# Both token halves of the next slice's gate and up projections ahead of each down-projection group, equal groups in both layers, and silu as one activation

## The chip, the cores and the metric

The kernel runs on one core of one Trainium2 chip. The metric is the device time of one execution in microseconds (us): the median of a few runs. Besides, one execution was recorded by the hardware profiler, and every row below is from that one. The engines are named as the profile names them: PE is the matrix engine (TensorE) and PEld its weight loads, DVE is VectorE, ACT is ScalarE, POOL is GpSimd, SP is SyncE, which here does nothing but issue transfers.

## What is computed

Two layers of a diffusion trunk over 640 tokens (512 latent, 128 of context) of width 1024. In each layer a conditioning vector gives six rows of shifts, scales and gates (the modulation); three kinds of mixers follow, an output projection, and a feed-forward block:

```
m  = silu(c) @ w_mod + b_mod                       # 6 rows of 1024 per conditioning vector
x  = layernorm(ALPHA * x + gate1 * mixers(modulated x) @ w_out)
h2 = layernorm(x) * (1 + scale2) + shift2
y  = (silu(h2 @ w_gate) * (h2 @ w_up)) @ w_down     # inner width 2816
x  = layernorm(ALPHA * x + gate2 * y)
```

The modulation takes a row each for two conditioning vectors (latent and context tokens).

## The kernel before

**Tiling.** The inner width of the feed-forward block is cut into 22 slices of 128. A matrix product in fp32 is made of three PE instructions on high and low parts (`mm3`, lines 218 to 220). Weights come in by SP transfers of 512 KB into `wraw` (line 211); ACT makes the high part `whi` (line 205), DVE the low part `wlo` (line 206). There are eight slots for such weight pairs.

**One slice.** `gu_unit(f, h)` makes the gate and up projection of slice `f` for one half of the tokens: 256 tokens (h = 0) or 384 (h = 1), 48 matmuls into two PSUM banks `pg` and `pu`. Before, silu takes two steps: ACT writes sigmoid(pg) into `sg` (line 1184), DVE multiplies it by `pg` (line 1185). DVE then multiplies by `pu` (line 1186). Behind h = 1 ACT and DVE split the slice's `sg` (640 tokens) into `ah` and `al`, and the slice's down weights are fetched.

**One group.** The slices are worked in groups (`GROUPS`). Behind the gate and up projections of a group stand its down projections: `d_unit(gi, t, hs)` for token tiles t = 0 to 4, each of two column halves `dps` of 512 columns, 3 matmuls for each slice and half. A finished half is multiplied by a gate row (line 1086, `residual`) and added to the residual `xr` (line 1088 in the first group, 1090 in later ones). All matmul outputs rotate through eight PSUM banks, so a unit that wants a bank waits until what it held has been evicted.

**Gate rows.** The first down unit of a layer fetches them (`gates(1)`, line 1071) from `gd` in DRAM, which the modulation writes: `modulation` works through pieces of 128 x 512 of the modulation weights. For each piece SP fetches `wm` (line 282), DVE multiplies and sums it for one conditioning vector (line 308), POOL multiplies it for the other (line 312), and ACT sums that product (line 288). Behind the last piece of a part DVE forms `modV` (lines 318, 319) and POOL issues the write of `gd` (line 323). Part 5 is the gate of the feed-forward block.

**Order.** PE runs in the order in which the program lists the matmuls. Units are listed by hand; the modulation's pieces are woven in between by a planner (`Order`), which lets one pass per so many planned microseconds of PE work (the pace). The order on ACT, DVE, POOL and SP follows from that by a scheduler. Before, layer 0 works its own part 5 (16 pieces, pace 2.8) and then parts 0 to 4 of layer 1 (80 pieces, pace 3.4) during its feed-forward block; layer 1 works its own part 5 (16 pieces, pace 2.8) during its own.

Of the kernel before, what the change touches and what calls it, by code (L numbers as in the profile page):

```python
# [12 lines left out]
AF = mybir.ActivationFunctionType  # L13
ALU = mybir.AluOpType
# [3 lines left out]
T = 640  # L18
NK = 8
NFF = 22  # L20
GROUPS = (((0, 4), (4, 4), (8, 4), (12, 4), (16, 6)), ((0, 5), (5, 6), (11, 5), (16, 6)))
ALPHA = float((2 * L) ** 0.25)
EPS = 1e-5
P = dict(pf=(0,), hf=0, hf4=2, vr0=1.0, vr=3.0, ew=5, lm=(0, 0), beg=12.0, dve=7.9, pace0=2.8, pace1=2.8, pace2=(3.4, 2.8), r=6.5, b=6.5, lev=2.4, v=6.1, hn=2.9, mixm=6.0, co=3.5, rco=4.0, rcs=3.0, norm=3.0)
HALVES = ((0, 256), (256, 384))
HH = (slice(0, 512), slice(512, 1024))
SWAP16 = [i ^ 16 for i in range(32)]
# [7 lines left out]
class Slots:  # L35
# [46 lines left out]
    def again(self, t, name, shape, dt=F32):  # L82

        kind, i, _ = self.held.pop(id(t))
        return self.view(kind, i, name, shape, dt)
# [66 lines left out]
class Kernel:  # L152
# [114 lines left out]
    def modulation(self, l, which, pace, dve):  # L267

        nc = self.nc
        keep = self.tc.keep_in_program_order  # L270
        again = self.mem.again
        yield lambda: self.can(ax=5 if dve else 6)
        csb = [self.get("ax", "csb", (128, 512)) for _ in range(2)]
        wts = deque(self.get("ax", "wm", (128, 512)) for _ in range(3 if dve else 4))
        acc = self.const.tile([128, 6, 2, 2, NK], F32, name="acc", tag="acc", bufs=1)
        ahead, tails = deque(), deque()

        def load(h, n, k):
            wt = again(wts.popleft(), "wm", (128, 512))
            wts.append(wt)  # L280
            r0 = (which[n] * NK + k) * 128
            keep(nc.sync.dma_start(wt, self.a["w_modT"][l, r0:r0 + 128, h * 512:(h + 1) * 512]))
            ahead.append((h, n, k, wt))

        def finish_tails(left):
            while len(tails) > left:
                t, d = tails.popleft()
                keep(nc.scalar.activation(out=t, in_=t, func=AF.Copy, accum_out=d))  # L288

        for h in range(2):  # L290
            for s in range(2):
                csb[s] = again(csb[s], "csb", (128, 512))
                nc.sync.dma_start(csb[s], self.a["crow"][s, h * 512:(h + 1) * 512].unsqueeze(0).to_broadcast([128, 512]))
                j = again(wts.popleft(), "junk", (128, 512))
                wts.append(j)
                nc.scalar.activation(out=j, in_=csb[s], func=AF.Sigmoid)
                nc.vector.tensor_tensor(csb[s], csb[s], j, ALU.mult)
                yield -pace
            pieces = deque((h, n, k) for n in range(len(which)) for k in range(NK))
            for _ in range(len(wts) - 2):  # L300
                load(*pieces.popleft())
            while ahead:
                if pieces:
                    load(*pieces.popleft())
                yield -pace
                _, n, k, wt = ahead.popleft()
                d = [acc[:, n, h, s, k:k + 1] for s in range(2)]
                keep(nc.vector.scalar_tensor_tensor(self.jb, wt, 1.0, csb[0], ALU.mult, ALU.mult, accum_out=d[0]))  # L308
                if dve:
                    nc.vector.scalar_tensor_tensor(self.jb, wt, 1.0, csb[1], ALU.mult, ALU.mult, accum_out=d[1])  # L310
                else:
                    nc.gpsimd.tensor_tensor(wt, wt, csb[1], ALU.mult)  # L312
                    tails.append((wt, d[1]))
                    finish_tails(1)
            finish_tails(0)
        for n, w in enumerate(which):
            v = self.modV[:, l, w]
            nc.vector.tensor_tensor(v, acc[:, n, 0], acc[:, n, 1], ALU.add)
            nc.vector.tensor_tensor(v, v, self.bmf[:, l, w].unsqueeze(1).to_broadcast([128, 2, NK]), ALU.add)
            if w in (1, 4):  # L320
                nc.vector.tensor_scalar(v, v, 1.0, None, ALU.add)
            if w in (2, 5):
                nc.gpsimd.dma_start(self.gd[l, w // 3].rearrange("s (k f) -> f (s k)", f=128),
                                    v.rearrange("p s k -> p (s k)"))
        self.free(*csb, *wts)
        self.mark(("mod", l, which[-1]))
# [100 lines left out]
    def tm_out(self, l, g, t, ps, n):  # L427
        self.mark(("V", l, g, t), P["v"])
        for j in range(n):
# [29 lines left out]
    def mixers(self, l, hT, mp):  # L459
        nc, a, o = self.nc, self.a, self.o  # L460
# [31 lines left out]
        hn = [[("hT", l, 0), ("hT", l, 1)], [("hT", l, 2), ("hT", l, 3), ("hT", l, 4)]]  # L492
# [50 lines left out]
        def e_unit(i, h):  # L543
            ps = half(15 + i, h, "pgt", 0)
            c0, n = HALVES[h]
            if h == 0:
                self.sg[i] = self.m4("sg", (128, T))
            sg = self.sg[i]
            nc.scalar.activation(out=sg[:, c0:c0 + n], in_=ps[:, :n], func=AF.Sigmoid)
            nc.vector.tensor_tensor(sg[:, c0:c0 + n], sg[:, c0:c0 + n], ps[:, :n], ALU.mult)  # L550
            if h:
                nc.vector.tensor_tensor(sg, sg, self.raws[i], ALU.mult)
                self.free(self.raws[i])
                m = 5 + i if i < 3 else i - 1
                self.mix[m] = (self.ax("mh"), self.ax("ml"))
                self.split(sg, *self.mix[m])
                self.free(sg)
                self.mark(("mix", l, m), P["mixm"])
# [497 lines left out]
    def feed(self, l, fp):  # L1056
        nc, a, o = self.nc, self.a, self.o
# [104 lines left out]
        par1 = []  # L1162

        def later_modulation():
            yield lambda: ("gu", l, P["lm"][l]) in self.at
            if l == 0:
                yield from self.modulation(0, (5,), P["pace1"], False)
            yield from self.modulation(1, (5,) if l else range(5), P["pace2"][l], False)

        o.start(later_modulation())  # L1170
        hT = self.hts("hT") if l < L - 1 else None
        acts, wd, sgs, wgu = {}, {}, {}, {}
        hn = [[("h2", l, 0), ("h2", l, 1)], [("h2", l, 2), ("h2", l, 3), ("h2", l, 4)]]

        def gu_unit(f, h):
            if f not in wgu:
                wgu[f] = (self.loadw(a["w_gate"][l, f]), self.loadw(a["w_up"][l, f], eng=nc.gpsimd if f in P["pf"] else None))
                sgs[f] = fp.tile([128, T], F32, tag="sg", name="sg", bufs=1)
            c0, n = HALVES[h]
            pg = self.fm_half(wgu[f][0], h2, h, "pg")  # L1180
            pu = self.fm_half(wgu[f][1], h2, h, "pu")
            self.mark(("gu", l, f))
            sg = sgs[f][:, c0:c0 + n]
            nc.scalar.activation(out=sg, in_=pg[:, :n], func=AF.Sigmoid)
            nc.vector.tensor_tensor(sg, sg, pg[:, :n], ALU.mult)
            nc.vector.tensor_tensor(sg, sg, pu[:, :n], ALU.mult)
            if h:
                for w in wgu.pop(f):
                    self.free(*w)
                acts[f] = (self.ax("ah"), self.ax("al"))  # L1190
                self.split(sgs[f], *acts[f])
                wd[f] = self.loadw(a["w_down"][l, f * 128:(f + 1) * 128, :])

        def d_unit(gi, t, hs):
            f0, n = GROUPS[l][gi]
            if not g2:
# [9 lines left out]
            if t == 4 and 1 in hs:  # L1206
                for f in range(f0, f0 + n):
                    self.free(*wd.pop(f), *acts.pop(f))
            final = gi == len(GROUPS[l]) - 1
            with self.tc.high_priority(offset=2000 if final else 0):  # L1210
# [14 lines left out]
        def gu(f, h):  # L1225
            self.unit(lambda: gu_unit(f, h), hn[h] + ([("gu", l, f)] if h else []), 5.2 if h == 0 else 7.8,
                      {"W": 2} if h == 0 else {"ax": 2})

        for gi, (f0, n) in enumerate(GROUPS[l]):


            if gi == 0 or l:
                gu(f0, 0)
            gu(f0, 1)
            for f in range(f0 + 1, f0 + n):
                for h in range(2):
                    gu(f, h)
            if gi < len(GROUPS[l]) - 1:
                if l == 0:
                    gu(f0 + n, 0)  # L1240
                for t in range(5):
                    self.unit(lambda gi=gi, t=t: d_unit(gi, t, (0, 1)), [("mod", l, 5)], 0.0)
                self.run_units(ahead=4 if gi == 0 else 1)
        self.run_units(ahead=1)
        gi = len(GROUPS[l]) - 1
        if l < L - 1:
# [238 lines left out]
```

## Time and profile before

| | |
|---|---|
| median of three runs | 1785.79 us (1784.29 to 1786.83) |
| the profiled execution, whole | 1783.5 us |
| its span, first to last instruction | 1781.7 us |
| mean granted TensorE clock over the span | 0.983 of full speed |
| PE busy | 1690.5 us, 95% of the span |
| DVE, ACT, POOL busy | 64%, 38%, 25% |

The profiled execution lies 2.3 us under the median. Its first gate projection starts at 433.3 us in layer 0 and at 1297.3 us in layer 1. An engine's busy share over the whole span does not say what an edit is worth; what PE waits for in the stretch that the edit touches does.

### The profile page before, as it was taken

The numbers are of one execution on the slowest core, as the hardware profiler recorded it, in microseconds if no ns is written. First come the engines' busy times: TensorE is split into PE (matmuls) and PEld (weight loads), VectorE is DVE, ScalarE is ACT, GpSimd is POOL, SyncE is SP. The second block draws the span as 40 slices with busy tenths as digits, with TensorE's granted clock in tenths as the row PEclk, the third lists the DMA queues.
The fourth block names the chain that finished last, engine by engine and source line by source line (L and its number), as shares of the span: only waits on it lengthen the run. The fifth ranks groups of instructions, "written<-read, shape, count | busy, mean of one in ns | idle before, by whom it ended". The sixth has DMA issues, their size and how long they took to land.

```text
span 1781.7 us, 29207 instructions
## 1 busy us (share of the span) xinstructions
PE 1690.5 (95%) x11634; PEld 1548.7 (87%) x11634; DVE 1134.1 (64%) x1979; ACT 671.3 (38%) x1277; POOL 452.4 (25%) x461
## 2 busy tenths in 40 slices
PE   6989879999888999999999999999999899999998
PEld 4878778888878999989989998879798799898996
DVE  4497897658657775877394546675767533434427
ACT  4623332735433443434254434256354122221310
POOL 2223342103253443543042333220233100000001
PEclk9999989999999999999999999999999899999999
DMA  8444521243345453544223122113244332221311
GB/s 327 156 131 132 144 61 40 81 166 95 102 147 166 154 166 119 174 122 154 72 82 120 60 62 69 40 58 117 100 137 146 108 103 71 73 84 47 106 36 59
DMA packets 71497, 195.47 MB, mean 110 GB/s; under 512 B 11953, under 2 KB 12737, under 8 KB 71361
## 3 DMA queue, kind: packets, MB, share of 16 engines
q1 hardware_dynamic: 67392, 183.15, 32.3%
q0 software_dynamic: 3680, 10.35, 1.8%
q8 instruction: 91, 1.49, 0.3%
q14 instruction: 46, 0.37, 0.1%
q10 hardware_dynamic: 288, 0.11, 0.0%
HBM read 187.52 MB, written 6.06 MB: 109 GB/s over the span
## 4 chain that ended last, share of the span: by engine, by line
PE 56%; DVE 5%; issue 3%; ACT 2%; DMA 2%; POOL 1%; DVEq 0%; ACTq 0%; POOLq 0%
PE dps L220 5%; PE dps L219 5%; PE dps L218 5%; PE pg L220 4%; PE pg L219 4%; PE pg L218 4%; PE pu L218 4%; PE pu L220 4%; PE pu L219 4%; PE pl L819 1%; PE p L218 1%; PE p L220 1%; PE p L219 1%; DVE jb L308 1%; DVE wlo L206 1%
## 5 line engine op out<-in xcount | busy, mean ns | idle before, releaser
L206 DVE TENSOR_TENSOR wlo<-wraw,whi 128x1024 fp32r<-128x1024 f32 x204 | 262.0, 1287 | 228.0 <-ACT whi L205 226.9
L205 ACT CAST whi<-wraw 128x1024 fp32r<-128x1024 f32 x206 | 215.3, 1048 | 431.7 <-PE pg L219 110.0
L312 POOL TENSOR_TENSOR wm<-wm,csb 128x512 f32<-128x512 f32 x112 | 182.4, 1644 | 263.9 <-DVE jb L308 255.3
L220 PE MATMUL pg<-h2T,wlo 128*128 128x384 f32 (+1 forms) x704 | 218.4, 310 | 2.4 <-DVE wlo L206 2.4
L218 PE MATMUL pg<-h2T,whi 128*128 128x384 f32 (+1 forms) x704 | 218.7, 311 | 0.0
L219 PE MATMUL pg<-h2T,whi 128*128 128x384 f32 (+1 forms) x704 | 218.0, 310 | 0.0
L218 PE MATMUL pu<-h2T,whi 128*128 128x384 f32 (+1 forms) x704 | 217.6, 309 | 0.0
L220 PE MATMUL pu<-h2T,wlo 128*128 128x384 f32 (+1 forms) x704 | 217.6, 309 | 0.0
L219 PE MATMUL pu<-h2T,whi 128*128 128x384 f32 (+1 forms) x704 | 217.6, 309 | 0.0
L218 PE MATMUL dps<-whi,ah 128*128 128x512 f32 x440 | 175.3, 399 | 17.0 <-ACT ah L205 11.7
L220 PE MATMUL dps<-whi,al 128*128 128x512 f32 x440 | 174.7, 397 | 3.4 <-DVE al L206 3.4
L219 PE MATMUL dps<-wlo,ah 128*128 128x512 f32 x440 | 174.4, 396 | 0.0
L334 POOL TENSOR_SCALAR bnve<-bnag 128x1 f32<-128x1 f32 x40 | 14.7, 371 | 596.3 <-DVE bnag L332 521.8
L308 DVE SCALAR_TENSOR_TENSOR jb<-wm,csb 128x512 bf16<-128x512 f32 x160 | 154.1, 963 | 11.2 <-DMA wm<-in_w_modT 9.3
L288 ACT ACTIVATE wm<-wm 128x512 f32<-128x512 f32 x112 | 70.7, 631 | 189.8 <-POOL wm L312 189.7
L220 PEld LDWEIGHTS pg<-h2T,wlo 128*128 128x128 f32 x704 | 134.0, 190 | 3.0 <-DVE wlo L206 3.0
L218 PEld LDWEIGHTS pg<-h2T,whi 128*128 128x128 f32 x704 | 134.1, 191 | 0.3
L219 PEld LDWEIGHTS pg<-h2T,whi 128*128 128x128 f32 x704 | 134.1, 190 | 0.3
L218 PEld LDWEIGHTS pu<-h2T,whi 128*128 128x128 f32 x704 | 133.8, 190 | 0.0
L219 PEld LDWEIGHTS pu<-h2T,whi 128*128 128x128 f32 x704 | 133.8, 190 | 0.0
L220 PEld LDWEIGHTS pu<-h2T,wlo 128*128 128x128 f32 x704 | 133.8, 190 | 0.0
L1086 DVE TENSOR_TENSOR dps<-dps,gate 128x512 f32<-128x512 f32 x90 | 60.8, 695 | 101.1 <-PE dps L220 71.1
(270 smaller groups left out, 3854.2 us busy)
## 6 DMA issues: line engine op xcount, KB each, us to landing
wm<-in_w_modT SPq DMA_DIRECT2D x160, 256.0 KB, 2.9
wraw<-in_w_gate SPq DMA_DIRECT2D x44, 512.0 KB, 3.6
wraw<-in_w_up SPq DMA_DIRECT2D x44, 512.0 KB, 3.7
wraw<-in_w_down SPq DMA_DIRECT2D x44, 512.0 KB, 3.6
wraw<-in_w_fm SPq DMA_DIRECT2D x42, 512.0 KB, 3.6
wm<-in_w_mod SPq DMA_DIRECT2D x16, 512.0 KB, 10.2
wraw<-in_w_tm SPq DMA_DIRECT2D x16, 512.0 KB, 3.7
wraw<-in_w_out SPq DMA_DIRECT2D x16, 512.0 KB, 3.7
```

Source lines behind the costliest of these rows:

```text
L205: self.nc.scalar.copy(hi, raw)
L206: (eng or self.nc.vector).tensor_tensor(lo, raw, hi.bitcast(F32), ALU.subtract)
L218: mm(out, lh, rh, start=first, stop=False)
L219: mm(out, lh, rl, start=False, stop=False)
L220: mm(out, ll, rh, start=False, stop=last)
L288: keep(nc.scalar.activation(out=t, in_=t, func=AF.Copy, accum_out=d))
L308: keep(nc.vector.scalar_tensor_tensor(self.jb, wt, 1.0, csb[0], ALU.mult, ALU.mult, accum_out=d[0]))
L312: nc.gpsimd.tensor_tensor(wt, wt, csb[1], ALU.mult)
L334: nc.gpsimd.tensor_scalar(ve, ag[:, 1:2], EPS, None, ALU.add)
L819: nc.tensor.matmul(pl[hh][:, u * 128:(u + 1) * 128], C[p0:p0 + 64, u * 128:(u + 1) * 128], pick(Qf, p0, p0 + 64, u * 128, [[2 * s, 64 // s ...
L1086: nc.vector.tensor_tensor(ps, ps, gt[:, HH[h]], ALU.mult)
```

## The change

Three things are done at once.

1. **Order and groups.** In both layers both halves of the next group's first slice now stand ahead of a group's down projections; before, layer 0 had only h = 0 there, and layer 1 neither. Layer 1 takes layer 0's groups, 4, 4, 4, 4 and 6 slices in place of 5, 6, 5 and 6.
2. **Modulation.** Part 5 of layer 1 is worked in layer 0 as well. Layer 0 now weaves in 16 + 96 pieces, the last 96 at a pace of 3.0, and layer 1's feed-forward block none.
3. **Silu.** ACT makes silu in one activation, in place of sigmoid on ACT and a multiplication on DVE, at three places: the gate projection, the mixers' output gates (`e_unit`) and the conditioning vector in the modulation that is woven in.

```diff
-GROUPS = (((0, 4), (4, 4), (8, 4), (12, 4), (16, 6)), ((0, 5), (5, 6), (11, 5), (16, 6)))
+GROUPS = (((0, 4), (4, 4), (8, 4), (12, 4), (16, 6)), ((0, 4), (4, 4), (8, 4), (12, 4), (16, 6)))
...
-P = dict(pf=(0,), hf=0, hf4=2, vr0=1.0, vr=3.0, ew=5, lm=(0, 0), beg=12.0, dve=7.9, pace0=2.8, pace1=2.8, pace2=(3.4, 2.8), r=6.5, b=6.5, lev=2.4, v=6.1, hn=2.9, mixm=6.0, co=3.5, rco=4.0, rcs=3.0, norm=3.0)
+P = dict(pf=(0,), hf=0, hf4=2, vr0=1.0, vr=3.0, ew=5, lm=0, beg=12.0, dve=7.9, pace0=2.8, pace1=2.8, pace2=3.0, r=6.5, b=6.5, lev=2.4, v=6.1, hn=2.9, mixm=6.0, co=3.5, rco=4.0, rcs=3.0, norm=3.0)
...
-                j = again(wts.popleft(), "junk", (128, 512))
-                wts.append(j)
-                nc.scalar.activation(out=j, in_=csb[s], func=AF.Sigmoid)
-                nc.vector.tensor_tensor(csb[s], csb[s], j, ALU.mult)
+                if dve:
...
+                else:
+                    nc.scalar.activation(out=csb[s], in_=csb[s], func=AF.Silu)
...
-            nc.scalar.activation(out=sg[:, c0:c0 + n], in_=ps[:, :n], func=AF.Sigmoid)
-            nc.vector.tensor_tensor(sg[:, c0:c0 + n], sg[:, c0:c0 + n], ps[:, :n], ALU.mult)
+            nc.scalar.activation(out=sg[:, c0:c0 + n], in_=ps[:, :n], func=AF.Silu)
...
-            yield lambda: ("gu", l, P["lm"][l]) in self.at
+            yield lambda: ("gu", l, P["lm"]) in self.at
             if l == 0:
                 yield from self.modulation(0, (5,), P["pace1"], False)
-            yield from self.modulation(1, (5,) if l else range(5), P["pace2"][l], False)
-
-        o.start(later_modulation())
+                yield from self.modulation(1, range(6), P["pace2"], False)
+
+        if l == 0:
+            o.start(later_modulation())
...
-            nc.scalar.activation(out=sg, in_=pg[:, :n], func=AF.Sigmoid)
-            nc.vector.tensor_tensor(sg, sg, pg[:, :n], ALU.mult)
+            nc.scalar.activation(out=sg, in_=pg[:, :n], func=AF.Silu)
             nc.vector.tensor_tensor(sg, sg, pu[:, :n], ALU.mult)
...
-            if gi == 0 or l:
-                gu(f0, 0)
-            gu(f0, 1)
-            for f in range(f0 + 1, f0 + n):
+            ending = gi == len(GROUPS[l]) - 1
+            for f in range(f0 + (gi > 0), f0 + n + (not ending)):
                 for h in range(2):
                     gu(f, h)
-            if gi < len(GROUPS[l]) - 1:
-                if l == 0:
-                    gu(f0 + n, 0)
+            if not ending:
                 for t in range(5):
```

**PE, layer 0, in front of the first down projection.** Each row is one instruction with its line, its output, its inputs and the output's shape. Before, the last matmuls ahead of it are those of slice 4's first half (256 columns):

```order
L218 MATMUL pu<-h2T_4040,whi 128x256
L219 MATMUL pu<-h2T_4041,whi 128x256
L220 MATMUL pu<-h2T_4040,wlo 128x256
L218 MATMUL dps<-whi,ah 128x512
L219 MATMUL dps<-wlo,ah 128x512
L220 MATMUL dps<-whi,al 128x512
```

Of the change, at the same place:

```order
L218 MATMUL pu<-h2T_4028,whi 128x384
L219 MATMUL pu<-h2T_4029,whi 128x384
L220 MATMUL pu<-h2T_4028,wlo 128x384
L218 MATMUL dps<-whi,ah 128x512
L219 MATMUL dps<-wlo,ah 128x512
L220 MATMUL dps<-whi,al 128x512
```

The 48 matmuls of slice 4's second half moved from behind the group's down projections to ahead of them; the number of matmuls in the program is the same.

**DVE, layer 0, in front of the first eviction of a down projection** (`dps<-dps,gate`). Before:

```order
L206 TENSOR_TENSOR wlo<-wraw,whi 128x1024
L206 TENSOR_TENSOR al<-sg,ah 128x640
L1185 TENSOR_TENSOR sg<-sg,pg 128x256
L1186 TENSOR_TENSOR sg<-sg,pu 128x256
L308 SCALAR_TENSOR_TENSOR jb,acc<-wm,csb 128x512 x3
L297 TENSOR_TENSOR csb<-csb,junk 128x512
L318 TENSOR_TENSOR modV<-acc 128x16
L319 TENSOR_TENSOR modV<-modV,bmf 128x16
L297 TENSOR_TENSOR csb<-csb,junk 128x512
L1086 TENSOR_TENSOR dps<-dps,gate 128x512 x2
L1088 SCALAR_TENSOR_TENSOR xr<-xr,dps 128x512 x2
```

Of the change (its line numbers are 2 or 3 higher there):

```order
L206 TENSOR_TENSOR wlo<-wraw,whi 128x1024
L206 TENSOR_TENSOR al<-sg,ah 128x640
L1188 TENSOR_TENSOR sg<-sg,pu 128x256
L311 SCALAR_TENSOR_TENSOR jb,acc<-wm,csb 128x512 x3
L321 TENSOR_TENSOR modV<-acc 128x16
L322 TENSOR_TENSOR modV<-modV,bmf 128x16
L206 TENSOR_TENSOR wlo<-wraw,whi 128x1024
L1188 TENSOR_TENSOR sg<-sg,pu 128x384
L206 TENSOR_TENSOR wlo<-wraw,whi 128x1024
L206 TENSOR_TENSOR al<-sg,ah 128x640
L1088 TENSOR_TENSOR dps<-dps,gate 128x512 x2
L1090 SCALAR_TENSOR_TENSOR xr<-xr,dps 128x512 x2
```

The same three pieces still stand behind slice 4's first half and ahead of `modV`; the multiplications by `pg` and by `junk` are gone, and slice 4's second half, its split and two weight splits stand between `modV` and the first eviction.

**SP, layer 1, ahead of the gate rows.** Before:

```order
L211 DMA wraw<-in_w_gate 128x1024
L282 DMA wm<-in_w_modT 128x512 x3
L211 DMA wraw<-in_w_up 128x1024
L211 DMA wraw<-in_w_down 128x1024
L293 DMA csb<-in_crow 128x512 x2
L282 DMA wm<-in_w_modT 128x512 x8
L211 DMA wraw<-in_w_gate 128x1024
L211 DMA wraw<-in_w_up 128x1024
L1071 DMA gate<-gd 128x1024 x2
```

Of the change:

```order
L211 DMA wraw<-in_w_down 128x1024 x4
L211 DMA wraw<-in_w_gate 128x1024
L211 DMA wraw<-in_w_up 128x1024
L211 DMA wraw<-in_w_down 128x1024
L1073 DMA gate<-gd 128x1024 x2
L1081 DMA ln_g<-in_ln_g 128x1024
L1081 DMA ln_b<-in_ln_b 128x1024
```

The modulation's transfers left this stretch, and the gate rows follow weights alone.

## Rows read from the trace of the kernel before

**Rows 1.** Windows: from:to, length, busy time by engine (instructions), granted clock, DMA, GB/s.

```profile
506.80:550.10 43.30, 32.19 (x122) 25.31 (x122) 23.39 (x43) 9.29 (x23) 15.48 (x11) 0.84 0.42 130
550.10:882.00 331.90, 331.62 (x2050) 316.77 (x2050) 234.27 (x376) 133.68 (x265) 129.08 (x80) 1.00 0.46 143
1370.90:1417.90 47.00, 37.91 (x152) 30.30 (x151) 26.32 (x42) 11.39 (x23) 14.09 (x9) 0.85 0.33 104
1417.90:1773.10 355.20, 355.20 (x2144) 334.95 (x2142) 159.33 (x227) 72.14 (x97) 7.47 (x12) 1.00 0.23 75
1387.00:1393.00 6.00, 6.00 (x14) 4.75 (x15) 1.97 (x4) 1.44 (x4) 3.60 (x3) 0.50 0.04 16
```

**Rows 2.** Timeline, PE, layer 0's first down group: start, length, instruction, wait and releaser.

```profile
515.29 0.50 PE L218 MATMUL dps<-whi,ah 128*128 128x512 f32 x1 [4.15 <-ACT ah L205]
517.70 0.80 PE L220 MATMUL dps<-whi,al 128*128 128x512 f32 x1 [1.62 <-DVE al L206]
...
536.01 0.39 PE L218 MATMUL dps<-whi,ah 128*128 128x512 f32 x1
...
536.69 0.39 PE L218 MATMUL dps<-whi,ah 128*128 128x512 f32 x1
...
542.88 0.80 PE L218 MATMUL dps<-whi,ah 128*128 128x512 f32 x1 [5.34 <-DVE xr L1088]
```

**Rows 3.** Timeline, PE, layer 1's first down group.

```profile
1384.24 0.79 PE L218 MATMUL dps<-whi,ah 128*128 128x512 f32 x1 [7.56 <-ACT ah L205]
...
1386.99 0.79 PE L220 MATMUL dps<-whi,al 128*128 128x512 f32 x1 [1.53 <-DVE al L206]
```

**Rows 4.** Timeline, DVE and ACT, just ahead of those.

```profile
1378.48 2.33 DVE L206 TENSOR_TENSOR wlo<-wraw,whi 128x1024 fp32r<-128x1024 f32 x1 [1.09 <-ACT whi L205]
...
1382.85 0.63 ACT L288 ACTIVATE wm<-wm 128x512 f32<-128x512 f32 x1 [1.43 <-POOL wm L312]
...
1383.48 0.71 ACT L205 CAST ah<-sg 128x640 fp32r<-128x640 f32 x1
```

**Rows 5.** Timeline, PE, a second half's gate and up projection, seven matmuls apart.

```profile
485.67 0.34 PE L219 MATMUL pu<-h2T,whi 128*128 128x384 f32 x1
...
486.88 0.34 PE L220 MATMUL pu<-h2T,wlo 128*128 128x384 f32 x1
```

**Rows 6.** The chain that ended last, in layer 0's first down group.

```profile
526.07 9.21 DMA gd<-modV
...
535.30 5.54 DMA gate<-gd
...
540.94 1.30 DVE dps L1086 x2
```

**Rows 7.** Timeline, DVE, layer 0, between the last pieces of part 5.

```profile
508.14 1.22 DVE L206 TENSOR_TENSOR wlo<-wraw,whi 128x1024 fp32r<-128x1024 f32 x1
...
514.64 2.27 DVE L206 TENSOR_TENSOR wlo<-wraw,whi 128x1024 fp32r<-128x1024 f32 x1 [1.17 <-ACT whi L205]
...
518.15 0.42 DVE L1185 TENSOR_TENSOR sg<-sg,pg 128x256 f32<-128x256 f32 x1 [0.51 <-ACT sg L1184]
...
521.51 0.69 DVE L308 SCALAR_TENSOR_TENSOR jb<-wm,csb 128x512 bf16<-128x512 f32 x1 [1.06 <-DMA wm<-in_w_modT]
```

**Rows 8.** Groups by line and shape: count, busy us, mean ns, idle time before and releaser.

```profile
L1185 DVE TENSOR_TENSOR sg<-sg,pg 128x384 f32<-128x384 f32 x44 | 24.1, 548 | 6.7 <-ACT sg L1184 6.7
L1185 DVE TENSOR_TENSOR sg<-sg,pg 128x256 f32<-128x256 f32 x44 | 18.5, 420 | 19.5 <-ACT sg L1184 19.5
L1184 ACT ACTIVATE sg<-pg 128x384 f32<-128x384 f32 x44 | 21.2, 482 | 7.1 <-PE pg L220 7.1
L308 DVE SCALAR_TENSOR_TENSOR jb<-wm,csb 128x512 bf16<-128x512 f32 x160 | 154.1, 963 | 11.2 <-DMA wm<-in_w_modT 9.3
L312 POOL TENSOR_TENSOR wm<-wm,csb 128x512 f32<-128x512 f32 x112 | 182.4, 1644 | 263.9 <-DVE jb L308 255.3 <-DMA wm<-in_w_modT 4.8 <-ACT whi L205 1.7
L549 ACT ACT_TABLE_LOAD x5 | 6.4, 1283 | 0.1
```

More of the change, by code (lines that the diff above doesn't have):

```diff
@@ L293, in modulation @@
                 nc.sync.dma_start(csb[s], self.a["crow"][s, h * 512:(h + 1) * 512].unsqueeze(0).to_broadcast([128, 512]))
-                j = again(wts.popleft(), "junk", (128, 512))
-                wts.append(j)
-                nc.scalar.activation(out=j, in_=csb[s], func=AF.Sigmoid)
-                nc.vector.tensor_tensor(csb[s], csb[s], j, ALU.mult)
+                if dve:
+                    j = again(wts.popleft(), "junk", (128, 512))
+                    wts.append(j)
+                    nc.scalar.activation(out=j, in_=csb[s], func=AF.Sigmoid)
+                    nc.vector.tensor_tensor(csb[s], csb[s], j, ALU.mult)
+                else:
+                    nc.scalar.activation(out=csb[s], in_=csb[s], func=AF.Silu)
                 yield -pace
```

## The prediction

> **What bounds the kernel now.** PE is busy 95% of the span, so I read first where the other 5% lies in the stretches that the edit touches, then what PE waits for there, and last what is late behind that.
>
> The windows show it [rows 1]. From 550 us to 882 us, most of layer 0's feed-forward block, PE is busy 331.62 of 331.90 us; in layer 1 from 1417.9 us to the end of the last down projections it is busy throughout. Nothing can be won there by moving work. The loss lies in one place of each layer, the first group of down projections. Such a matmul costs 0.227 us at full clock: three lie between 536.01 and 536.69 [rows 2]. Layer 0's first group has 4 slices x 5 tiles x 2 halves x 3 = 120 of them, 27.2 us, but its window lasts 43.3 us: 16.1 us are lost. Layer 1's has 5 slices, 150 matmuls, 34.0 us, and its window lasts 47.0 us: 13.0 us are lost.
>
> In layer 0 the reader sees three waits [rows 2]: 4.15 us for the high part `ah` of the last slice, 1.62 us for its low part `al`, and 5.34 us for an eviction, 11.1 us together. The other 5.0 us are clock: after a wait the matmuls come further apart; the last tile, from 542.88 to the window's end at 550.10, takes 7.2 us for 24 x 0.227 = 5.4 us of work. In layer 1 there are two waits, 7.56 and 1.53 us [rows 3], and behind them a stretch at half the clock (0.50, the 1.2 GHz level of the two) [rows 1]; 13.0 less 9.1 leaves 3.9 us to it.
>
> Why is `ah` late? In layer 1 the ACT cast of `ah` starts at 1383.48, when ACT ends the sum of a modulation piece that had itself waited for POOL [rows 4], and DVE, which must finish `sg` ahead of that cast, had its weight split drawn out to 2.33 us, against 1.22 us where no POOL work lies beside it [rows 4, 7]. So modulation pieces sit on the last slice's chain just when PE has nothing but the down projections left. The eviction wait of layer 0 is another chain [rows 6]: the write of the gate row takes 9.21 us from 526.07, its load 5.54 us from 535.30, and DVE's first eviction starts at 540.94. By then four tiles fill all eight PSUM banks.
>
> **Layer 1: 13.0 us won.** No modulation piece is left in this layer, and ahead of the first down projection of the last slice (3 now) stand both halves of slice 4 and three slices of down projections. A second half's projection alone is 48 matmuls at 0.173 us (seven between 485.67 and 486.88 [rows 5]), 8.3 us, and nothing but weight splits competes with the cast and the split of slice 3. The gate rows follow weights on SP, and their row of `gd` was written a layer earlier. Both waits go, and the slow clock behind them. I take all 13.0; the lower bound, 11.0, leaves one wait of the size of 1.53 us with some slow clock. The one group more costs ten further halves to evict and add up, two DVE instructions each of some 0.65 us (1.30 for two [rows 6]), 13 us of DVE in all; DVE is busy 159 of 355 us there [rows 1], and PE has 5.4 us for a tile. I take zero; without that cover it would be 13.
>
> **Layer 0: 9.9 us won.** Before, PE ended slice 4's first half at 506.8 and went into the down projections. Now slice 4's second half fills 506.8 to 515.1. The down projections then need `ah` and `al` of slice 3 only 18 matmuls later, at 519.2, and in the trace of before `al` was there at 517.7 [rows 2]. Both waits (5.8 us) go. Four tiles later, at 515.1 + 4 x 5.44 = 536.9, the banks are full, and PE waits for the first eviction as before. What is late next is therefore the gate row.
>
> Before, PE went on at 542.88, 1.94 us after DVE's start at 540.94 [rows 2, 6]. Ahead of `modV` on DVE the multiplications by `pg` (0.42 and 0.55 us [rows 8]) and the 0.51 us in which DVE waited for ACT in front of one of them [rows 7] go; I let the gate come by their sum, 1.5 us, earlier: eviction 539.4, PE 541.4, a wait of 4.5 us, then the last tile at the 7.2 us of before: its end is at 548.6. Before, the same work (the group and slice 4's second half) ended at 550.1 + 8.3 = 558.4. Gain 9.8, with rounding 9.9. Bounds: 4.2 us earlier than before (the 1.06 us wait for `wm` [rows 7] and one piece's POOL time of 1.64 us [rows 8] go as well), gain 12.5; 1.6 us later (nothing saved, and one piece's POOL time more), gain 6.7. On DVE two weight splits and the second half's `al` now stand ahead of the first eviction; 2 x 1.23 + 0.82 + 0.55 us fit between 526 and 539.
>
> **The rest at zero.** Silu on ACT I price as the sigmoid that it replaces, 482 ns for 384 columns; even twice that hides, since ACT is busy 134 of 332 us in layer 0 [rows 1, 8]. The multiplications that go from DVE (0.55 and 0.42 us, 44 each) lie beside a busy PE. The order of ACT has one table load more, 28 for 27: between 0 and 1.28 us [rows 8], zero taken because ACT is ahead of PE in most stretches. The start of layer 0's block could win up to 1.7 us from a shorter DVE queue; zero taken. The pieces in layer 0 come denser. In the window of 332 us POOL's 129 us are some 79 pieces; at a pace of 3.0 for 3.4 it is 89.5. DVE gets 10.5 x 0.96 = 10.1 us more and, for 16 slices, 15.5 us less: 229 of 332 us. POOL goes to 146. Zero taken, since PE lost 0.28 us there; its bound is the rivals' matter.
>
> **Sum.** 1783.5 - 13.0 - 9.9 = 1760.6 us against the profiled execution. The median stands 2.3 us above that, so 1762.9, called 1763. With all bounds together (27.2 and 16.4 us won) it is 1759 to 1769.
>
> **Rivals.**
> - *Layer 0's stall goes entirely* (0.08). If the gate row lands six microseconds earlier (539.4 turned into 535.0), PE never waits: 16.1 + 13.0 = 29.1, 1757. For it: the 9.21 us of the write is the longest piece of the chain. Against: its write and load stay as they are, and on DVE the split of slice 4 stands ahead.
> - *The gate is later* (0.07). Two conditioning loads and four pieces' loads still stand ahead of it on SP. Four microseconds after before, 544.9, leave a gain of 4.3 in layer 0: 1768.
> - *A new wait in layer 0* (0.11). The denser pieces make one `ah` or weight late behind a later group, as they did in layer 1 at a pace of 2.8. By the size of that, 7.56 + 1.53 = 9.1 us [rows 3]: 1772. Against it speaks that at 3.4 there was none from 550 to 882.
> - *The moved pieces are not hidden* (0.05), which ends slower. DVE and POOL hinder each other: the split took 2.27 us with POOL at work and 1.22 without [rows 7], and a DVE piece takes 0.96 us on average against 0.69 at 521.51 [rows 7, 8]. If each of the 16 pieces that come into layer 0 costs PE its POOL time, 16 x 1.64 = 26.3 us, the gain of 22.9 is more than eaten: 1789. It decides from 22.9 / 16 = 1.43 us for each piece. Against: 79 such pieces cost 0.28 us in the window. The Trainium skill (SBUF — State Buffer, Who interferes with whom) says that DVE and GpSimd share one pair of ports as an exclusive lock, and that a DVE instruction with two SBUF inputs contends with a GpSimd one that reads SBUF. The trace agrees by the 2.27 us.
> - *The stalls only move* (0.03): the gate row in layer 0 and the weights in layer 1, the next in line, give back what `ah` no longer takes. Within 3.6 us of before, so about 1784.
>
> **How the numbers follow.** The case of the sum has 0.66; it and the first three rivals end faster, 0.92 in all; the moved stall is 0.03 of no change, the unhidden pieces 0.05 slower. About 0.2%, 3.6 us, is what a measurement of this kernel can tell from none. The range goes from 1755, under the stall-free case, to 1773, over the case of the new wait; the two cases beyond hold 0.08.
>
> **What would show it.** Right: in layer 1's first down group no wait for `ah` or `al`, and a window of 27.2 us for 4 slices at full clock. In layer 0 slice 4's second half ends near 515, no wait for `ah`, and one wait of about 4.5 us for an eviction ahead of the fifth tile, with a slow stretch behind it. DVE's first eviction near 539. Wrong: waits of PE for `wlo`, `ah` or `al` after 550 us, a stretch between 550 and 882 with PE under 99%, or a gate that lands later than 541.

## The result, and the profile after

The changed kernel takes 1763.78 us (median of three runs, 1760.22 to 1764.48) against 1785.79 us: ratio 0.9872, 95% interval 0.9854 to 0.9891. The forecast was 1763. Two repeats gave 1763.29 (0.9873, interval 0.9855 to 0.9891) and 1762.38 (0.9860, interval 0.9844 to 0.9877).

The profiled execution has a span of 1758.4 us, 23.3 less than before. To say where the 23.3 us came from, the span is cut at the same work in both kernels: layer 0's first gate projection, the end of slice 4's first half, and the end of the first group of down projections together with slice 4's second half. Windows of before (from:to, length, busy time by engine, granted clock, DMA, GB/s):

```profile
433.30:506.87 73.57, 66.80 (x455) 66.36 (x454) 49.41 (x75) 38.45 (x72) 23.74 (x19) 0.95 0.46 146
506.87:558.42 51.55, 40.44 (x170) 33.52 (x169) 31.49 (x55) 13.18 (x31) 19.52 (x13) 0.87 0.42 132
```

And of the change, with the rest of layer 0's slices and layer 1's block (the fifth row is layer 1's first group of down projections):

```profile
432.10:502.21 70.11, 66.48 (x456) 65.80 (x454) 43.84 (x64) 38.52 (x72) 23.83 (x18) 0.98 0.47 145
502.21:547.62 45.41, 38.52 (x170) 32.74 (x169) 25.49 (x45) 12.46 (x28) 15.88 (x10) 0.89 0.48 157
547.62:880.00 332.38, 332.38 (x2044) 316.24 (x2043) 231.02 (x374) 141.80 (x293) 150.91 (x97) 1.00 0.52 153
1287.20:1400.00 112.80, 112.65 (x708) 107.62 (x707) 58.38 (x79) 40.64 (x63) 7.95 (x7) 1.00 0.35 116
1360.07:1387.30 27.23, 27.23 (x121) 22.53 (x121) 15.41 (x22) 3.79 (x4) 0.00 (x0) 1.00 0.11 38
1400.00:1748.50 348.50, 348.50 (x2083) 327.42 (x2083) 149.34 (x204) 68.34 (x92) 7.47 (x12) 1.00 0.22 69
```

For layer 1 the cuts are the last matmul of the output projection (`ops`) and the last of the down projections (`dps`): first and last start stand in the view of a tile. Of before, then of the change:

```profile
L218 PE MATMUL ops<-whi,mh x160: 387/390/478, 376.4 to 1296.2; 128*128 128x512 f32 x160
L218 PE MATMUL dps<-whi,ah x440: 387/390/797, 506.9 to 1772.4; 128*128 128x512 f32 x147
```

```profile
L218 PE MATMUL ops<-whi,mh x160: 387/389/478, 375.4 to 1286.3; 128*128 128x512 f32 x160
L218 PE MATMUL dps<-whi,ah x440: 387/389/796, 510.5 to 1748.5; 128*128 128x512 f32 x147
```

| stretch | forecast gain | measured |
|---|---|---|
| up to layer 0's block | 0 | 433.3 - 432.1 = 1.2 |
| start of layer 0's block, to slice 4's first half | 0 | 73.57 - 70.11 = 3.5 |
| first down group with slice 4's second half | 9.9 | 51.55 - 45.41 = 6.1 |
| from there to layer 1's output projection | 0 | 737.8 - 738.7 = -0.9 |
| layer 1's feed-forward block | 13.0 | 476.2 - 462.2 = 14.0 |
| behind the last down projections | 0 | 9.3 - 9.9 = -0.6 |
| sum | 22.9 | 23.3 |

In layer 1 PE waits nowhere in its down groups. Its first group takes 27.23 us, busy throughout at full clock, where 27.2 was forecast and where before 13.0 us were lost [rows 1, 3]; from 1400.00 us on PE is busy 348.50 of 348.50 us. In layer 0 the two waits for `ah` and `al` [rows 2] are gone, and one wait is left, for the first eviction (timeline, PE, of the change):

```profile
539.39 0.80 PE L218 MATMUL dps<-whi,ah 128*128 128x512 f32 x1 [6.89 <-DVE xr L1090]
```

The chain that ended last shows the gate row behind it, as before [rows 6]:

```profile
520.48 10.81 DMA gd<-modV
...
531.31 6.05 DMA gate<-gd
...
537.45 1.30 DVE dps L1088 x2
```

The write takes 10.81 us for 9.21, the load 6.05 for 5.54. Silu costs ACT what sigmoid did: 481 ns for 384 columns against 482 [rows 8].

### The profile page after: what moved, and what is told of

Same layout as the page of the kernel before. It is cut to its first block, busy times and chain, and to the rows that moved or that the text cites. A ratio compares the mean times of both kernels' runs of the same rounds, so it can differ in the third digit from the quotient of the medians.

```text
span 1758.4 us, 29068 instructions
## 1 busy us (share of the span) xinstructions
PE 1687.5 (96%) x11634; PEld 1548.5 (88%) x11634; DVE 1081.7 (62%) x1875; ACT 671.2 (38%) x1274; POOL 447.2 (25%) x461
## 4 chain that ended last, share of the span: by engine, by line
PE 76%; DVE 10%; issue 3%; DMA 3%; ACT 3%; POOL 2%; DVEq 0%; SPq 0%; ACTq 0%; POOLq 0%
PE pg L220 5%; PE pu L219 5%; PE pu L218 5%; PE pg L219 5%; PE pu L220 5%; PE pg L218 5%; PE dps L218 5%; PE dps L219 5%; PE dps L220 5%; PE pl L821 2%; PE p L218 2%; DVE jb L311 2%; PE p L220 2%; PE p L219 2%; PE ops L220 2%
## 5 line engine op out<-in xcount | busy, mean ns | idle before, releaser
L315 POOL TENSOR_TENSOR wm<-wm,csb 128x512 f32<-128x512 f32 x112 | 177.9, 1610 | 211.0 <-DVE jb L311 198.3
L311 DVE SCALAR_TENSOR_TENSOR jb<-wm,csb 128x512 bf16<-128x512 f32 x160 | 145.8, 911 | 29.1 <-DMA wm<-in_w_modT 27.0
L1088 DVE TENSOR_TENSOR dps<-dps,gate 128x512 f32<-128x512 f32 x100 | 67.6, 695 | 75.1 <-PE dps L220 63.8
```

Source lines behind the costliest of these rows:

```text
L1088: nc.vector.tensor_tensor(ps, ps, gt[:, HH[h]], ALU.mult)
```

## The experiments

**Three parts, one at a time, and the change without one.** The theory (A): layer 0's stall ends by the order, layer 1's by the removal of the pieces, and silu brings only what the start of layer 0's block shows. The rivals: the relief of DVE ended the stalls (B), or the slice that now stands ahead ended both (C).

*Silu alone.* Before, with the three silu hunks of the change.

```diff
-            nc.scalar.activation(out=sg, in_=pg[:, :n], func=AF.Sigmoid)
-            nc.vector.tensor_tensor(sg, sg, pg[:, :n], ALU.mult)
+            nc.scalar.activation(out=sg, in_=pg[:, :n], func=AF.Silu)
```

> Before with the silu edit alone (one activation at the three places; order, groups and modulation as before). Theory A (the first groups' stalls end by the order in layer 0 and by the pieces' removal in layer 1; silu is worth only what the start of layer 0's feed-forward block showed, 3.4 us, and up to 1.5 us on the way to the gate row): 1781 to 1783 us, PE still waits about 7.5 us for ah in layer 1's first group of down projections. Theory B (DVE relief is what ended the stalls): 1768 to 1773, no wait for ah over 2 us in either layer.

Measured: 1778.54 us (median of 5), ratio 0.9956, interval 0.9943 to 0.9970. That is more than A expected and far from B. Timeline, PE:

```profile
512.48 0.79 PE L218 MATMUL dps<-whi,ah 128*128 128x512 f32 x1 [4.91 <-ACT ah L205]
...
1379.95 0.79 PE L218 MATMUL dps<-whi,ah 128*128 128x512 f32 x1 [7.75 <-ACT ah L205]
```

Both waits for `ah` stand as before [rows 2, 3], so B is out. What A had not expected lies in layer 1: its block, cut as above, takes 1765.8 - 1292.8 = 473.0 us for 476.2, and PE no longer waits there for `al` (1.53 us before), nor for a low part of a weight at the block's start (1.0 us in two waits before).

*Order alone.* Before, with the groups and the order of the change, which no run takes apart; sigmoid, and part 5 of layer 1 in layer 1. `GROUPS` is changed besides the lines shown.

```diff
-            if gi == 0 or l:
-                gu(f0, 0)
-            gu(f0, 1)
-            for f in range(f0 + 1, f0 + n):
+            ending = gi == len(GROUPS[l]) - 1
+            for f in range(f0 + (gi > 0), f0 + n + (not ending)):
                 for h in range(2):
                     gu(f, h)
-            if gi < len(GROUPS[l]) - 1:
-                if l == 0:
-                    gu(f0 + n, 0)
+            if not ending:
```

> Before with the order and the groups of the change alone (sigmoid and multiplication, part 5 of layer 1 still in layer 1). Theory A: layer 0 gains about 6 us; in layer 1 ah is covered, but the gate row is late next: eviction near 1407 as before, PE reaches the fifth tile at 1393, a wait of about 16 us for an eviction, so layer 1 gains nothing or loses up to 5 us; 1780 to 1786 us in all. Theory C (the slice that now stands ahead is what ended layer 1's stall): 1766 to 1769, no wait over 2 us in layer 1.

Measured: 1785.52 us (median of 11), ratio 1.0002, interval 0.9991 to 1.0012: no gain at all. Timeline, PE and DVE:

```profile
547.38 0.79 PE L218 MATMUL dps<-whi,ah 128*128 128x512 f32 x1 [11.20 <-DVE xr L1088]
...
1402.49 1.30 DVE L1086 TENSOR_TENSOR dps<-dps,gate 128x512 f32<-128x512 f32 x2 [15.42 <-DMA gate<-gd]
...
1404.43 0.80 PE L218 MATMUL dps<-whi,ah 128*128 128x512 f32 x1 [15.48 <-DVE xr L1088]
```

No wait for `ah` is left, and the gate row takes its place in both layers, 15.48 us in layer 1 where about 16 was expected. That is A's reading: a stall that is covered uncovers the next. In layer 0, though, the first group with slice 4's second half gained 2.5 us (49.1 for 51.55) and not 6: a weight of 512 KB was issued beside the write of the gate row, and the write took 14.2 us in place of 9.2. Layer 1's block became 4.6 us longer (480.8 for 476.2), within what A allowed.

*Modulation alone.* Before, with part 5 of layer 1 in layer 0 and all 96 pieces at a pace of 3.0, where 80 had 3.4.

```diff
-            yield from self.modulation(1, (5,) if l else range(5), P["pace2"][l], False)
-
-        o.start(later_modulation())
+                yield from self.modulation(1, range(6), P["pace2"], False)
+
+        if l == 0:
+            o.start(later_modulation())
```

> Before with the modulation edit alone (part 5 of layer 1 worked in layer 0 at a pace of 3.0, none in layer 1; old order, groups and silu). Theory A: layer 1's stall goes without the new order, 13 us, layer 0's first group loses its 16 us as before: 1772 to 1774 us. Theory C: layer 1 still waits for ah, 1783 to 1787. The unhidden pieces, if there are any, would show as waits of PE between 550 and 880 us and a time above 1780.

Measured: 1788.36 us (median of 11), ratio 1.0016, interval 1.0006 to 1.0026. A's number is wrong by 15 us. The tile rows say where:

```profile
L218 PE MATMUL ops<-whi,mh x160: 387/389/478, 376.8 to 1315.0; 128*128 128x512 f32 x160
L218 PE MATMUL dps<-whi,ah x440: 387/389/794, 507.4 to 1777.8; 128*128 128x512 f32 x147
```

Layer 1's block takes 1777.8 - 1315.0 = 462.8 us for 476.2, so the 13 us are won there, and C is out. But layer 1 starts 18.8 us later: layer 0 pays for the pieces. Timeline, PE:

```profile
615.60 0.79 PE L218 MATMUL dps<-whi,ah 128*128 128x512 f32 x1 [3.96 <-ACT ah L205]
...
617.32 0.80 PE L220 MATMUL dps<-whi,al 128*128 128x512 f32 x1 [0.50 <-DVE al L206]
...
883.44 0.58 PE L218 MATMUL pu<-h2T,whi 128*128 128x256 f32 x1 [5.22 <-ACT whi L205]
```

One is the wait that layer 1 had, now at the second group of layer 0; slow clock follows both (0.50 granted from 615.60 to 622.00 us, 0.61 from 884.00 to 890.00). The other has a cause of its own. Transfers issued from 866 to 884 us (KB, us to landing):

```profile
wraw<-in_w_up SPq DMA_DIRECT2D x1, 512.0 KB, 14.0
wraw<-in_w_down SPq DMA_DIRECT2D x1, 512.0 KB, 12.9
gd<-modV POOLq DMA_DIRECT2D x1, 8.0 KB, 14.4
```

The write of layer 1's gate rows, at 866.79 us (850.40 in the change), met the last weights: they landed after 14.0 and 12.9 us, where such a transfer takes 3.6 in the median of the kernel before.

*The change without silu.*

> The change with sigmoid and multiplication in place of silu (order, groups and modulation as changed). Theory A: 3 to 5 us above the change, 1767 to 1769 us, by a longer wait for xn or a weight at the start of layer 0's block and a later gate row. Theory B: 1775 or more, with waits for ah or al back.

Measured: 1769.41 us (median of 4), ratio 0.9899, interval 0.9883 to 0.9915. Its edit is that of silu alone, reversed in the change at all three places. Waits of PE from 430 to 900 us (total, times, longest):

```profile
PE dps L218 <- DVE xr L1088: 12.0, 1, 12.0
PE lnT L365 <- ACT xn L354: 4.6, 1, 4.6
PE pg L220 <- DVE wlo L206: 1.4, 1, 1.4
```

No `ah`, no weight behind 550 us: with the new order the pieces in layer 0 are hidden without silu too. What silu is worth here, 6 us by the medians and 4.6 by the ratios, is at the start and on the gate row (12.0 against 6.9).

*The change without the order.* Old order and groups, silu and moved pieces kept: the edit of order alone, reversed.

> The change with the old order and groups (silu and moved modulation stay). Theory D (the slice that stands ahead is what covers the denser pieces in layer 0; without it they cost, as they did with the modulation moved alone): 1776 to 1782 us, waits for ah or a weight between 550 and 890 us in layer 0, none in layer 1. Theory E (with silu the pieces are hidden in the old order too): 1768 to 1771 us, no such waits, and layer 0's first group loses about 12 to 16 us as before.

Measured: 1773.53 us (median of 5), ratio 0.9932, interval 0.9920 to 0.9945, between D and E. Timeline, PE:

```profile
511.48 0.79 PE L218 MATMUL dps<-whi,ah 128*128 128x512 f32 x1 [5.06 <-ACT ah L205]
...
538.48 0.80 PE L218 MATMUL dps<-whi,ah 128*128 128x512 f32 x1 [5.82 <-DVE xr L1090]
...
607.87 0.50 PE L218 MATMUL dps<-whi,ah 128*128 128x512 f32 x1 [1.76 <-ACT ah L205]
```

The wait at the second group is back, but 1.76 us in place of 3.96. So silu hides most of the pieces in the old order, and the order hides the rest; the order is worth some 10 us within the change, though nothing by itself. The two profiled executions are 13.7 us apart: 6.3 lie in layer 0's first group with slice 4's second half, 7.3 behind it, up to layer 1's output projection.

**The stall that is left.** *The change again*, for comparison on the same chip.

> The changed kernel itself, for a comparison on one chip with the next three: 1760 to 1765 us, one wait of 6 to 8 us for an eviction in layer 0's first group of down projections.

Measured: 1763.29 us (median of 5), with a wait of 7.8 us for the eviction.

*Part 5 faster.*

```diff
-pace1=2.8
+pace1=1.5
```

> The change with layer 0's own part 5 at a pace of 1.5 in place of 2.8, so that its modV stands ahead of slice 4's first half on DVE. If the chain of the gate row (last piece, write, load) alone sets the wait that is left: first eviction 4 to 8 us earlier, the wait of 6.9 us shrinks to 0 to 3, 1754 to 1760 us. If the denser pieces make ah or a weight late instead: that wait shows ahead of the first group and the time stays at 1761 to 1766.

Measured: 1764.40 us (median of 4), ratio 0.9886, interval 0.9873 to 0.9900. Timeline, PE:

```profile
536.30 0.50 PE L218 MATMUL dps<-whi,ah 128*128 128x512 f32 x1 [4.30 <-ACT sg L1187]
...
538.96 0.79 PE L218 MATMUL dps<-whi,ah 128*128 128x512 f32 x1 [1.70 <-DVE sg L1188]
```

PE no longer waits for an eviction there, but for the banks that silu and its product have not yet emptied. The time is that of the second expectation; the waits are neither, since they are not for `ah` or a weight and stand inside the group. Timeline, DVE and ACT, say why silu was late:

```profile
531.35 0.69 DVE L311 SCALAR_TENSOR_TENSOR jb<-wm,csb 128x512 bf16<-128x512 f32 x1 [8.38 <-DMA wm<-in_w_modT]
...
533.92 0.63 ACT L288 ACTIVATE wm<-wm 128x512 f32<-128x512 f32 x1 [7.81 <-POOL wm L315]
```

DVE waited 8.38 us for the load of a piece, and ACT had the sums of these pieces ahead of slice 4's last silu, which it began at 535.78. Four loads of pieces issued beside the write of the gate row landed after 7.1 to 10.8 us, where 3.0 is the median of that run.

*The write from ACT's queue.*

```diff
-                nc.gpsimd.dma_start(self.gd[l, w // 3].rearrange("s (k f) -> f (s k)", f=128),
+                nc.scalar.dma_start(self.gd[l, w // 3].rearrange("s (k f) -> f (s k)", f=128),
```

> The change with the write of the gate rows issued from ACT's queue in place of POOL's, all else equal. If the write's 9 to 11 us come from the queue that issues it: first eviction some 3 to 6 us earlier, 1756 to 1760 us. If they come from its many small pieces: the write lands as late as before (within 1 us), 1760 to 1765; ACT's issue may delay a cast by about 1 us.

Measured: 1761.87 us (median of 4), ratio 0.9883, interval 0.9867 to 0.9899, and the eviction's wait is 8.0 us. Transfers beside the write, by issue:

```profile
wraw<-in_w_gate SPq DMA_DIRECT2D x1, 512.0 KB, 12.6
gd<-modV ACTq DMA_DIRECT2D x1, 8.0 KB, 14.5
```

The write landed after 14.5 us, where POOL's took 10.8 in the change. The two are not alike, since here a weight was issued beside it and there none; POOL's writes with a weight beside took 13.1 to 15.9 us. Like for like is the earlier write near 191 us, with the same transfers issued around it: 11.9 us from ACT, 11.8 to 12.9 from POOL in the other runs. The queue that issues it is not the reason.

*Half a slice more ahead.* Slice 5's first half also stands ahead of layer 0's first down group.

```diff
                 for h in range(2):
-                    gu(f, h)
+                    if (l, f, h) != (0, 5, 0):
+                        gu(f, h)
+            if (l, gi) == (0, 0):
+                gu(f0 + n + 1, 0)
```

> The change with slice 5's first half (48 matmuls, 5.7 us) also ahead of layer 0's first group of down projections. If the wait that is left is set by the gate row's arrival alone: the wait of 7 to 8 us shrinks to 1 to 3 us and the half clock behind it to 0 to 2.8, 1754 to 1759 us, 5 to 9 us under the change in the same call. If the gate row comes later by as much (its chain follows PE's progress): the wait stays at 6 to 8 us and the time within 3 us of the change.

Measured: 1762.15 us (median of 4), ratio 0.9860, interval 0.9840 to 0.9880, beside 1762.38 for the change. Neither expectation: the wait for the eviction is gone, yet the time is that of the change. Timeline, PE and ACT:

```profile
519.74 0.58 PE L218 MATMUL pu<-h2T,whi 128*128 128x256 f32 x1 [5.81 <-ACT whi L205]
```

```profile
518.03 0.63 ACT L288 ACTIVATE wm<-wm 128x512 f32<-128x512 f32 x1 [0.50 <-POOL wm L315]
...
518.65 1.03 ACT L205 CAST whi<-wraw 128x1024 fp32r<-128x1024 f32 x1
```

Slice 5's up weights are now needed earlier, and ACT casts them behind the last sums of part 5, which wait for POOL.

> The changed kernel once more, beside half_slice_more: 1760 to 1765 us.

Measured: 1762.38 us (median of 4), with a wait of 6.9 us for the eviction.

*Those weights earlier too.* Slice 5's weights are fetched and split at slice 4's first half.

```diff
+            if (l, f, h) == (0, 4, 0):
+                wgu[5] = (self.loadw(a["w_gate"][l, 5]), self.loadw(a["w_up"][l, 5]))
...
-             {"W": 2} if h == 0 else {"ax": 2})
+             {"W": 2 if (l, f) != (0, 5) else 0} if h == 0 else {"ax": 2})
```

> half_slice_more with slice 5's gate and up weights also fetched and split a unit earlier, at slice 4's first half, so that ACT casts the up weights ahead of the last four sums of part 5. If the wait for that cast (5.8 us and a slow stretch) is all that half_slice_more exchanged for the eviction's: no wait over 1 us is left in layer 0 from 460 to 900 us, 1752 to 1757 us, 5 to 10 us under the change. If the gate row or slice 3's down weights, now cast later, take its place: a wait for an eviction or for a weight of 3 to 8 us shows in the first group and the time stays at 1759 to 1764.

Measured: 1757.96 us (median of 4), ratio 0.9855, interval 0.9835 to 0.9875. One wait is left in the first group (timeline, PE):

```profile
541.93 0.62 PE L218 MATMUL dps<-whi,ah 128*128 128x512 f32 x1 [3.14 <-DVE xr L1090]
```

The time lies just above the first expectation, and the wait is one that the second named: the gate row still sets what is left.

> The same kernel as half_slice_weights_early, once more, since its interval overlaps that of the change: 1756 to 1760 us if it is some 5 us under the change, 1760 to 1765 if the two are equal.

Measured: 1758.32 us (median of 5), ratio 0.9848, interval 0.9830 to 0.9866. The nine runs of this version lie between 1754.28 and 1759.43 us, the twelve of the change between 1756.21 and 1765.80; the medians are 5 us apart and ten of the twelve lie above all nine, while the intervals of the ratios overlap. By its median it is the fastest version here.

## Why the prediction was right, point by point

- **What bounds the kernel.** Right in the main: nothing was won where PE had been busy throughout. But the loss did not lie "in one place of each layer" alone: at the start of layer 0's block PE was busy 66.80 of 73.57 us, and some of that was won.
- **Layer 1, 13.0 us.** Right, measured 14.0. That it is the removal of the pieces that counts is shown from both sides: with the pieces still there the order alone left 15.48 us to the gate row, and with the pieces gone the old order won 13.4 us in that layer. The slices that stand ahead, which the prediction named beside it, were not needed there. The 1.0 us above the forecast lies ahead of the first group: from the first gate projection to the first down projection it was 73.76 us and is 72.76.
- **Layer 0, 9.9 us: mis-sized, 6.1**, under the lower bound of 6.7 (the sum's own rows give 9.8). The two waits for `ah` and `al` went as forecast, and what is late next is the gate row, as forecast. The step that failed is "I let the gate come 1.5 us earlier". Counted from the end of slice 4's first half, the first eviction came 35.2 us later (537.45 - 502.21) where before it came 34.1 (540.94 - 506.87); I had reckoned 32.6. The difference of 2.7 us has three parts. `modV` and the issue of the write came 0.9 us earlier (18.3 us behind that end for 19.2) and not 1.5: the wait of 0.51 us for ACT, which was to go with the multiplication, only moved to the next one (timeline, DVE, of the change):

```profile
513.16 0.42 DVE L1188 TENSOR_TENSOR sg<-sg,pu 128x256 f32<-128x256 f32 x1 [0.51 <-ACT sg L1187]
```

The write, which I had left at its old length, took 1.6 us more, and the load 0.5. So the wait is 6.89 us for 4.5. The last tile then takes 8.2 us (539.39 to 547.62) for 7.2, at a lower granted clock; windows over it, of before, then of the change:

```profile
542.88:550.10 7.22, 7.22 (x24) 5.86 (x25) 7.22 (x15) 0.72 (x2) 1.83 (x2) 0.75 0.18 62
```

```profile
539.39:547.62 8.23, 8.23 (x24) 6.58 (x25) 8.20 (x17) 0.72 (x2) 2.88 (x2) 0.65 0.49 193
```

Transfers beside the write, by issue (KB each, us to landing), of before:

```profile
wm<-in_w_modT SPq DMA_DIRECT2D x2, 256.0 KB, 3.7
gd<-modV POOLq DMA_DIRECT2D x1, 8.0 KB, 9.2
```

Of the change:

```profile
wm<-in_w_modT SPq DMA_DIRECT2D x3, 256.0 KB, 5.0
...
gd<-modV POOLq DMA_DIRECT2D x1, 8.0 KB, 10.8
```

Of silu alone:

```profile
wm<-in_w_modT SPq DMA_DIRECT2D x1, 256.0 KB, 3.3
gd<-modV POOLq DMA_DIRECT2D x1, 8.0 KB, 9.0
```

Of the change without silu:

```profile
wraw<-in_w_gate SPq DMA_DIRECT2D x1, 512.0 KB, 12.7
...
gd<-modV POOLq DMA_DIRECT2D x1, 8.0 KB, 15.9
```

Over all fourteen profiled executions this write in layer 0's first group took 13.1 to 15.9 us in the six where a weight of 512 KB was issued within 2 us behind it, and 9.0 to 11.1 in the others. Which transfers fall beside it follows from the order on SP. That a weight beside it lengthens the write is read from these rows, not from a run that changed the traffic alone. For the 1.6 us of the change, which has no weight beside, the cause stays open: five transfers lay beside its write and two beside that of before, but in layer 1 of the kernel before the write took 10.1 us with none:

```profile
gd<-modV POOLq DMA_DIRECT2D x1, 8.0 KB, 10.1
```

- **The rest at zero.** The start of layer 0's block won 3.5 us, above its bound of 1.7, and so made up for most of what layer 0's first group lacked: the total is closer than its terms. This gain is silu's, but not a steady one. The stretch from the first gate projection to the end of slice 4's first half lasts 69.95 to 71.25 us in seven profiled executions with silu and 73.02 to 73.86 in three, and 73.37 to 73.82 in the four without. One of the three is the change itself, run again, and won nothing there; that the profiled execution of the change was of the short kind is luck. In all three PE waits longer for an `xn` of the layer normalization, 2.2 to 5.0 us against 1.1 in the change, but silu alone, of the short kind, waits 2.5; the cause stays open. It may be part of why the change's runs scatter over 10 us.
- **The rivals.** "Layer 0's stall goes entirely" did not come. "The gate is later" is partly what happened. "A new wait in layer 0" and "The stalls only move" did not come in the change; the second is what the order did alone. "The moved pieces are not hidden", to which I gave 0.05, was nearer than the number says: with the modulation moved alone they cost layer 0 some 19 us, more than the 13.4 that layer 1 gains. Its argument against, 79 pieces at a cost of 0.28 us, did not carry over to denser pieces; that the order itself would cover them, and silu most of them without it, I had not seen. In the change PE is busy 332.38 of 332.38 us behind the first group, so the zero taken for them came true, but by luck as far as that argument goes. The extra table load cost nothing that can be found.

## What to carry to other kernels

Where a wait of PE is removed, what is late next can take its place, here the gate row for `ah` and a weight's cast for the gate row; price that one from its own chain before counting the first as won. Three edits that are worth 0.4%, nothing and less than nothing alone were worth 1.3% together, so an edit that shows no gain by itself is to be tried together with the one that covers what it uncovers.

## What was not expected of the hardware

The write of a gate row is 8 KB, and by the code neighbouring fp32 numbers of a partition go to addresses 512 bytes apart. In layer 0's first down group it took 9.0 to 15.9 us, and 14.5 when ACT's queue issued it with a weight beside. In that group, and at the end of layer 0 with the modulation moved alone, transfers of 512 KB issued within 4 us behind such a write took 12.6 to 14.8 us against a median of 3.6. With no transfer beside it the write still took 10.1 us (layer 1 of the kernel before). In the stretch around one such write the DMA engines were busy 0.31 and 0.41 of the time while they moved 23 and 56 GB/s (windows of the kernel with the modulation moved alone):

```profile
868.00:874.00 6.00, 6.00 (x37) 6.00 (x36) 4.01 (x7) 1.46 (x3) 0.00 (x0) 1.00 0.31 23
874.00:880.00 6.00, 4.22 (x32) 4.01 (x30) 0.00 (x0) 0.00 (x0) 0.00 (x0) 1.00 0.41 56
```

The Trainium skill (DMA: Bandwidth & Descriptors, Why small descriptors are slow) gives small pieces to and from HBM a fixed cost each; the rows agree that such a write is slow, and show besides that large transfers beside it are held up.
